# Stick-breaking scores issued in pairs of heads, and a pooling product cut to the band

## The chip, the cores and the metric

The kernel runs on one core of a Trainium2 chip. The metric is the device time of one execution in microseconds (us), lower is better; the number given is the median of several runs. All matrix products are done in a split form: a float32 operand is written as a rounded high part and a low part (`hi`, `lo`), both in the reduced type that TensorE takes, and a product is the sum of three matmuls, high by high, high by low and low by high.

## The reference, cut to what matters

A trunk of four residual layers over 256 tokens of 1024 channels. Each layer has a token mixer (layers 0 and 3: pooling; layer 1: stick-breaking attention; layer 2: a state-space layer called S5), then cross-attention into a fixed memory, then a gated MLP. Two mixers matter here.

```python
def pool_mixer(h, w, scale):          # windows 2, 4, 8, 16 over four channel groups of 256
    for gi, win in enumerate(POOL_WINDOWS):
        win_sum = c - causal_shift(c, win)          # c: running sum over the tokens
        cnt = jnp.minimum(counts, float(win))
        groups.append(win_sum / cnt - hf[..., sl])
    ...
    y = einsum('bsgc,gcd->bsgd', p, w)              # then a per-group linear map and a scale

def stick_breaking_attention(h, w_qkv, w_o):        # 16 heads of 64 channels
    z = einsum('bqhd,bkhd->bhqk', q, k) * scale
    log_one_minus = where(mask, log_sigmoid(-z), 0) # mask: key before query
    between = reverse_cumsum(log_one_minus) - log_one_minus
    a = where(mask, exp(log_sigmoid(z) + between), 0)
    o = einsum('bhqk,bkhd->bqhd', a, v)
```

In the pooling mixer the window mean minus the token is a 256 by 256 matrix over the tokens, one for each window. Column t of it is nonzero only in rows t-15 to t, and its entries are 1/window except in the first 15 columns, where the count is smaller.

## The kernel before, in words

Everything is written as straight code by engine; the framework's scheduler then orders the instructions of each engine by its own estimate of when operands are ready, so code that is near in the program may be interleaved. Each engine runs its own list in order. Weights come from DRAM by `load` (line 79): one DMA of 1 MB into a `raw` tile, then in two halves a cast on ScalarE (ACT, line 70, `whi`) and a subtraction on VectorE (DVE) or, where `eng` says so, on GpSimd (POOL) (line 71, `wlo`). A product `mm3` (line 62) issues three matmuls; in the trace they are lines 65, 66 and 67.

**Pooling, layers 0 and 3** (`pool_mixer`, line 443). The normalised tokens `xh, xl` lie with tokens on the partitions, in two tiles `tt` of 128 tokens. `band` is the matrix above, split like a weight. For each of the four windows and two chunks of 128 channels, two `mm3` (one for each token tile, line 459) of 256 columns sum into half of a PSUM bank: 2 x 2 x 3 matmuls for a window, 48 for a layer. Two `split_scaled` (lines 75 and 76, tiles `ah` on ACT and `al` on DVE) take each bank out. Then 48 matmuls with `pool_w` fill `acc` (line 473), and lines 476 and 477 on DVE scale and add to the residual `h`. In layer 0 two things share the time of this stage: conversions of the convolution constants (lines 145 and 146) and the poles of the S5 layer (a sine and cosine, lines 623 to 657 on DVE in tiny steps, results copied at lines 697 and 698; a power on POOL, line 693). POOL also splits early weights of the cross-attention there.

**Stick-breaking, layer 1** (`stick_mixer`, line 480). Q and K are kept transposed, two heads to a chunk: head 2p in partitions 0 to 63, head 2p+1 in partitions 64 to 127 (`rows`, line 543). For a head, `scores` (line 541) issues six matmuls (line 551: two key tiles by three split terms, 64 rows, 128 stationary and 256 moving columns) into a bank `z`, one matmul that adds the mask (line 552), and then the chain of a head: three activations on ACT (lines 554 to 556), two DVE operations (lines 558 and 559) and a split into `Lh, Ll`. `sticks` (line 563) adds the sums over later keys to `z` with four matmuls (lines 566 and 568), takes the exponential and splits it into `Ah, Al`. `values` (line 573) does six matmuls for a pair of heads (line 581) into `po`. The loop at line 594 runs over head n: `scores(n)`, S5 work at a `fill` point, a projection that a later head needs (the table `order`, 48 matmuls each), `values` at odd n, `sticks(n-1)`. There are two buffers of `Lh, Ll, Ah, Al`, one for even and one for odd heads, and four banks for `z`.

```python
for n in range(SBH + 2):
    if n < SBH:
        zs[n] = scores(n)
    ...
    if n % 2 and n >= 3:
        values((n - 3) // 2)
    if 0 <= n - 1 < SBH:
        sticks(n - 1, zs[n - 1])
```

Of the kernel before, what the change touches and what calls it, by code (L numbers as in the profile page):

```python
# [8 lines left out]
F32 = mybir.dt.float32  # L9
F32R = mybir.dt.float32r  # L10
AF = mybir.ActivationFunctionType
ALU = mybir.AluOpType
AX = mybir.AxisListType

P = 128
T = 256
TT = T // P
# [8 lines left out]
SBH = 16  # L26
# [10 lines left out]
class Trunk:  # L37
# [405 lines left out]
    def pool_mixer(self, l, j, ctx_pool):  # L443
        nc = self.nc
        xs = self.norm_natural()
        xh, xl = self.act_pair(TT, D)
        for tt in range(TT):
            self.split(xh[:, tt, :], xl[:, tt, :], xs[:, tt, :])
        self.fill("mnorm")
        sc = self.bcast(ctx_pool, self.a["pool_scale"][j], "psc")  # L450
        band = self.load(self.a["band"], 8, T)
        ph, pl = self.act_pair()
        for g in range(4):
            ps = self.bank()
            for jj in range(2):
                c = 2 * g + jj
                s = slice(c * P, (c + 1) * P)
                for tt in range(TT):
                    self.mm3(ps[:, jj * T : (jj + 1) * T], (xh[:, tt, s], xl[:, tt, s]), band(2 * g + tt, slice(0, T)), tt == 0, tt == 1)
            for jj in range(2):  # L460
                c = 2 * g + jj
                self.split_scaled(ph[:, c, :], pl[:, c, :], ps[:, jj * T : (jj + 1) * T], self.gain("mix", l, c))
        w = self.load(self.a["pool_w"][j].rearrange("g (c p) n -> p (g c) n", p=P), 8, T)
        self.fill("pool")
        accs = self.accs()
        for gh in range(2):
            for tt in range(TT):
                ps = accs[2 * gh + tt]
                s = slice(tt * P, (tt + 1) * P)
                for gg in range(2):  # L470
                    for k in range(2):
                        c = 4 * gh + 2 * gg + k
                        self.mm3(ps[:, gg * T : (gg + 1) * T], (ph[:, c, s], pl[:, c, s]), w(c, slice(0, T)), k == 0, k == 1)
                t = ctx_pool.tile([P, 512], F32, tag="pt", name="pt", bufs=2)
                cs = slice(512 * gh, 512 * (gh + 1))
                nc.vector.tensor_mul(t[:], ps[:], sc[:, cs])
                nc.vector.tensor_add(self.h[:, tt, cs], self.h[:, tt, cs], t[:])
                self.residual_done(gh, tt, ps[:])

    def stick_mixer(self, l, sp):  # L480
        nc, tc = self.nc, self.tc
        mm = nc.tensor.matmul
# [9 lines left out]
        neg = sp.tile([P, 2 * P], F32R, name="neg")  # L492
        idr = sp.tile([P, P], F32R, name="idr")
# [11 lines left out]
        bufs = []  # L505
# [10 lines left out]
        qk = self.act_pair()  # L516
# [21 lines left out]
            self.split(f(V[0]), f(V[1]), ps[:].rearrange("p (t n) -> p t n", t=TT))  # L538


        def scores(head):
            pair = head // 2
            rows = slice(64 * (head % 2), 64 * (head % 2) + 64)
            qc = 2 * (pair // 2 % 2) + pair % 2
            Lh, Ll = bufs[head % 2][:2]
            z = self.psa.tile([P, 512], F32, tag=f"acc{head % 4}", name="z")
            for kt in (1, 0):
                out = z[:, 0:T] if kt else z[:, T : 2 * T]
                ks = slice(kt * P, (kt + 1) * P)
                for n, (a, b) in enumerate([(0, 0), (0, 1), (1, 0)]):  # L550
                    mm(out, qk[a][rows, 4 + qc, ks], qk[b][rows, qc, :], start=kt == 1 and n == 0, stop=False, skip_group_check=True)
            mm(z[:, P : 3 * P], idr[:], neg[:], start=False, stop=False, skip_group_check=True)
            ab = sp.tile([P, 384], F32, tag="ab", name="ab", bufs=4)
            nc.scalar.activation(ab[:], z[:, P:], AF.Abs, scale=0.125)
            nc.scalar.activation(ab[:], ab[:], AF.Exp, scale=-1.0)
            nc.scalar.activation(ab[:], ab[:], AF.Ln, bias=1.0)
            L = sp.tile([P, 384], F32, tag="ab", name="L", bufs=4)
            nc.vector.tensor_scalar(L[:], z[:, P:], -0.125, 0.0, ALU.mult, ALU.min)
            nc.vector.tensor_sub(L[:], L[:], ab[:])
            self.split(Lh[:, P:], Ll[:, P:], L[:])  # L560
            return z

        def sticks(head, z):
            Lh, Ll, Ah, Al = bufs[head % 2]
            for x in (Lh, Ll):
                mm(z[:, P:], tri[:], x[:, P:], start=False, stop=False, skip_group_check=True)
            for n, x in enumerate((Lh, Ll)):
                mm(z[:, T:], ones[:], x[:, :T], start=False, stop=n == 1, skip_group_check=True)
            A = sp.tile([P, 384], F32, tag="ab", name="A", bufs=4)
            nc.scalar.activation(A[:], z[:, P:], AF.Exp, scale=0.125)  # L570
            self.split(Ah, Al, A[:])

        def values(pair):

            po = self.bank("po")
            cs = slice(P * pair, P * (pair + 1))
            out = po[:].rearrange("p (e q) -> p e q", e=2)

            for kt, q0 in ((0, 0), (1, P)):
                for a, b in ((0, 0), (0, 1), (1, 0)):  # L580
                    mm(
                        out[:, :, q0:], V[a][:, kt, cs], AA[b][:, :, 0:P] if kt else AA[b][:, :, P:],
                        start=kt == 0 and a == b, stop=kt == 1 and a == 1, skip_group_check=True,
                    )
            for e in range(2):
                rows = slice(64 * e, 64 * e + 64)
                self.split(O[0][rows, pair, :], O[1][rows, pair, :], po[rows, T * e : T * (e + 1)])
# [4 lines left out]
        order = {0: "v0", 1: "q1", 3: "k1", 5: "v1", 6: "q2", 7: "k2", 9: "v2", 10: "q3", 11: "k3", 13: "v3"}  # L592
        zs = {}
        for n in range(SBH + 2):
            if n < SBH:
                zs[n] = scores(n)
            self.fill(f"head{n}")
            for unit in order.get(n, "").split():
                u = int(unit[1])
                proj_v(u) if unit[0] == "v" else proj(u, "qk".index(unit[0]))  # L600
            if n % 2 and n >= 3:
                values((n - 3) // 2)
            if 0 <= n - 1 < SBH:
                sticks(n - 1, zs[n - 1])
        self.project(self.a["sb_w_o"][0].rearrange("(c p) n -> p c n", p=P), O, self.add_residual)


# [752 lines left out]
def band():  # L1360

    import numpy as np

    t = np.arange(T)
    out = np.zeros((P, 4, TT, T), np.float32)
    for g, w in enumerate(WINDOWS):
        m = ((t[:, None] <= t[None, :]) & (t[:, None] > t[None, :] - w)) / np.minimum(t + 1, w)[None, :] - np.eye(T)
        out[:, g] = m.reshape(TT, P, T).transpose(1, 0, 2)
    return out.reshape(P, 4 * TT, T).astype(np.float32)
# [31 lines left out]
```

## Time and profile before

| | us |
|---|---|
| median of 3 runs | 1502.92 (1499.14 to 1503.51) |
| the profiled execution | 1504.49 |
| its span | 1502.8 |
| PE busy, of the span | 1436.3 (96%) |
| DVE busy | 1100.1 (73%) |
| ACT busy | 843.0 (56%) |

In the profile PE is TensorE's matmuls, PEld its weight loads, DVE VectorE, ACT ScalarE, POOL GpSimd. The busy time of PE holds the tails of matmuls that overlap the next ones, so what a matmul costs is read from the distance between starts, not from its duration. On the chain that ended last PE has 75% of the span, DVE 12%, DMA 7% and ACT 3%.

### The profile page before, as it was taken

What the parts mean: (1) busy time and instruction counts of PE and PEld (TensorE: products, weight loads), DVE (VectorE), ACT (ScalarE), POOL (GpSimd) and SP (SyncE); (2) the same over time, 40 slices, a digit from 0 to 9 for tenths busy, and PEclk for the clock granted to TensorE, in tenths of its full rate; (3) what the DMA queues carried; (4) which work ended last, traced back from release to release, by engine and by line L of the source; (5) the groups of instructions that cost most, each with busy time, mean ns of one, the idle gap of its engine ahead of it and who ended that gap; (6) DMA issues with size and microseconds to landing.
All of it is one profiled execution on the core that took longest, in us unless ns stands there. A gap on an engine that the chain in (4) does not pass through costs nothing.

```text
span 1502.8 us, 25420 instructions
## 1 busy us (share of the span) xinstructions
PE 1436.3 (96%) x10370; PEld 1325.5 (88%) x10370; DVE 1100.1 (73%) x1720; ACT 843.0 (56%) x1351; POOL 127.1 (8%) x128
## 2 busy tenths in 40 slices
PE   7999999999999999999997679999999999999997
PEld 7898999989998989999986558989999999899996
DVE  6969887867887577978772755868777686677775
ACT  6654656547785465645453245656555565465553
POOL 3401000000000000111116300000000030000000
PEclk9999999999999999999998889999999999999999
DMA  7666656635334645776758474546555464465551
GB/s 257 210 175 208 236 201 208 205 126 184 129 138 144 204 135 194 243 233 218 232 190 241 159 270 151 169 141 226 194 169 196 155 203 163 137 218 179 173 192 43
DMA packets 205682, 279.75 MB, mean 186 GB/s; under 512 B 23740, under 2 KB 163132, under 8 KB 203644
## 3 DMA queue, kind: packets, MB, share of 16 engines
q1 hardware_dynamic: 199420, 263.08, 53.1%
q0 software_dynamic: 6144, 15.04, 3.1%
q8 instruction: 81, 1.33, 0.4%
q14 instruction: 37, 0.30, 0.1%
HBM read 264.24 MB, written 16.94 MB: 187 GB/s over the span
## 4 chain that ended last, share of the span: by engine, by line
PE 75%; DVE 12%; DMA 7%; ACT 3%; issue 2%; SPq 0%; POOL 0%; DVEq 0%; POOLq 0%; ACTq 0%
PE u L66 9%; PE u L67 9%; PE u L65 9%; PE mm L66 7%; PE mm L65 7%; PE mm L67 7%; PE acc L66 6%; PE acc L65 6%; PE acc L67 6%; DMA raw<-in_ffn_w_up_dram 3%; DVE wlo L71 3%; DVE ug L1239 2%; ACT whi L70 1%; DMA raw<-in_s_w_glu_dram 1%; DMA bl<-blD 1%
## 5 line engine op out<-in xcount | busy, mean ns | idle before, releaser
L71 DVE TENSOR_TENSOR wlo<-raw,whi 128x1024 fp32r<-128x1024 f32 x428 | 517.2, 1221 | 157.4 <-ACT whi L70 151.2
L70 ACT CAST whi<-raw 128x1024 fp32r<-128x1024 f32 (+1 forms) x450 | 459.7, 1045 | 194.2 <-DMA raw<-in_ffn_w_up_dram 61.3
L65 PE MATMUL u<-ah,whi 128*128 128x256 f32 x1408 | 400.9, 285 | 2.4 <-DVE ug L1239 2.1
L66 PE MATMUL u<-al,whi 128*128 128x256 f32 x1408 | 400.2, 284 | 0.2 <-DVE al L71 0.2
L67 PE MATMUL u<-ah,wlo 128*128 128x256 f32 x1408 | 400.0, 284 | 0.0
L65 PEld LDWEIGHTS u<-ah,whi 128*128 128x128 f32 x1408 | 271.7, 193 | 6.9 <-issue 3.6
L66 PEld LDWEIGHTS u<-al,whi 128*128 128x128 f32 x1408 | 271.6, 193 | 3.1 <-DVE al L71 0.7
L67 PEld LDWEIGHTS u<-ah,wlo 128*128 128x128 f32 x1408 | 271.7, 193 | 0.0
L1239 DVE SCALAR_TENSOR_TENSOR ug<-u,cwT,ug 128x255 f32<-128x255 f32 x352 | 168.5, 480 | 102.0 <-ACT ug L1237 97.0
L1237 ACT ACTIVATE ug<-u,cwT 128x256 f32<-128x256 f32 x176 | 99.2, 563 | 182.4 <-PE u L67 120.3
L65 PE MATMUL acc<-whi,gg 128*128 128x512 f32 x352 | 138.0, 392 | 0.0
L66 PE MATMUL acc<-wlo,gg 128*128 128x512 f32 x352 | 137.9, 392 | 0.0
L67 PE MATMUL acc<-whi,gg 128*128 128x512 f32 x352 | 136.9, 389 | 0.0
L66 PE MATMUL mm<-al,whi 128*128 128x256 f32 x384 | 109.8, 286 | 0.1
L65 PE MATMUL mm<-ah,whi 128*128 128x256 f32 x384 | 109.7, 286 | 0.0
L67 PE MATMUL mm<-ah,wlo 128*128 128x256 f32 x384 | 109.3, 285 | 0.0
L176 POOL TENSOR_TENSOR r<-v,mhalf 128x1 f32<-128x1 f32 x28 | 21.4, 765 | 832.8 <-DVE v L172 679.4
L67 PEld LDWEIGHTS acc<-whi,gg 128*128 128x128 f32 x352 | 66.1, 188 | 14.3
L65 PEld LDWEIGHTS acc<-whi,gg 128*128 128x128 f32 x352 | 66.4, 189 | 11.7
L66 PEld LDWEIGHTS acc<-wlo,gg 128*128 128x128 f32 x352 | 66.4, 189 | 10.7
L66 PEld LDWEIGHTS mm<-al,whi 128*128 128x128 f32 x384 | 74.4, 194 | 0.8 <-DVE al L71 0.6
L65 PEld LDWEIGHTS mm<-ah,whi 128*128 128x128 f32 x384 | 74.4, 194 | 0.3 <-ACT ah L70 0.2
(348 smaller groups left out, 2605.9 us busy)
## 6 DMA issues: line engine op xcount, KB each, us to landing
raw<-in_ffn_w_up_dram SPq DMA_DIRECT2D x88, 1024.0 KB
raw<-in_ffn_w_down_dram SPq DMA_DIRECT2D x44, 1024.0 KB
raw<-in_xa_wkv_dram SPq DMA_DIRECT2D x30, 1024.0 KB
raw<-in_xa_wq_dram SPq DMA_DIRECT2D x16, 1024.0 KB
raw<-in_xa_wo_dram SPq DMA_DIRECT2D x16, 1024.0 KB
raw<-in_sb_w_qkv_dram SPq DMA_DIRECT2D x12, 1024.0 KB
raw<-in_s_w_glu_dram SPq DMA_DIRECT2D x8, 1024.0 KB
raw<-in_sb_w_o_dram SPq DMA_DIRECT2D x4, 1024.0 KB
```

What stands on the lines that cost most here:

```text
L65: mm(out, lh, rh, start=start, stop=False)
L66: mm(out, lh, rl, start=False, stop=False)
L67: self.multiplied = mm(out, ll, rh, start=False, stop=stop).ins
L70: x = self.nc.scalar.copy(hi, src)
L71: y = (eng or self.nc.vector).tensor_sub(lo, src, hi.bitcast(F32))
L176: self.powed = nc.gpsimd.tensor_tensor(r[:], v[:], self.mhalf[:], ALU.pow).ins
L1237: nc.scalar.activation(u[:, s, :], out, AF.Identity, bias=cw[3], scale=cw[2])
L1239: nc.vector.scalar_tensor_tensor(u[:, s, sh:], out[:, : T - sh], cw[2 - sh], u[:, s, sh:], ALU.mult, ALU.add)
```

## The change

**Pooling.** The three matmuls of 256 columns for each token tile go. For token tile 1 (rows 128 to 255) only columns 128 to 255 are computed, for tile 0 only columns 0 to 143, since the band is zero elsewhere. The product of the tokens with the low part of the band is kept only for the first 16 columns. The matmuls are still in the split form otherwise. A chunk takes 5 matmuls (128, 128, 144, 144 and 16 columns) where there were 6 of 256.

**Stick-breaking.** `scores` works on a pair of heads. It issues the twelve matmuls alternately, one of head 2p on partitions 0 to 63 and one of head 2p+1 on partitions 64 to 127, into two banks; then the mask and the chain of each head. It stops before the split of the second head's `L`, so that `sticks` of the odd head before, which reads the same buffer, is issued first. The loop's even steps hold the scores of two heads, the odd steps none.

```diff
@@ pool_mixer
-                for tt in range(TT):
-                    self.mm3(ps[:, jj * T : (jj + 1) * T], (xh[:, tt, s], xl[:, tt, s]), band(2 * g + tt, slice(0, T)), tt == 0, tt == 1)
+                mm = nc.tensor.matmul
+                for tt, t0, t1 in ((1, P, T), (0, 0, P + 16)):
+                    to = ps[:, jj * T + t0 : jj * T + t1]
+                    bh, bl = band(2 * g + tt, slice(t0, t1))
+                    mm(to, xh[:, tt, s], bh, start=tt == 1, stop=False, skip_group_check=True)
+                    mm(to, xl[:, tt, s], bh, start=False, stop=False, skip_group_check=True)
+                    if t0 == 0:
+                        mm(to[:, 0:16], xh[:, tt, s], bl[:, 0:16], start=False, stop=True, skip_group_check=True)
@@ stick_mixer
-        def scores(head):
-            pair = head // 2
-            rows = slice(64 * (head % 2), 64 * (head % 2) + 64)
+        def scores(pair):
             qc = 2 * (pair // 2 % 2) + pair % 2
-            Lh, Ll = bufs[head % 2][:2]
-            z = self.psa.tile([P, 512], F32, tag=f"acc{head % 4}", name="z")
+            zz = [self.psa.tile([P, 512], F32, tag=f"acc{(2 * pair + e) % 4}", name="z") for e in range(2)]
             for kt in (1, 0):
-                out = z[:, 0:T] if kt else z[:, T : 2 * T]
                 ks = slice(kt * P, (kt + 1) * P)
                 for n, (a, b) in enumerate([(0, 0), (0, 1), (1, 0)]):
-                    mm(out, qk[a][rows, 4 + qc, ks], qk[b][rows, qc, :], start=kt == 1 and n == 0, stop=False, skip_group_check=True)
-            mm(z[:, P : 3 * P], idr[:], neg[:], start=False, stop=False, skip_group_check=True)
+                    for e in range(2):
+                        out = zz[e][:, 0:T] if kt else zz[e][:, T : 2 * T]
+                        rows = slice(64 * e, 64 * e + 64)
+                        mm(out, qk[a][rows, 4 + qc, ks], qk[b][rows, qc, :], start=kt == 1 and n == 0, stop=False, skip_group_check=True)
+            for e, z in enumerate(zz):
+                Lh, Ll = bufs[e][:2]
+                mm(z[:, P : 3 * P], idr[:], neg[:], start=False, stop=False, skip_group_check=True)
...
+                if e:
+                    yield zz
+                self.split(Lh[:, P:], Ll[:, P:], L[:])
@@ the loop over n
-            if n < SBH:
-                zs[n] = scores(n)
+            if n % 2 == 0:
+                rest = scores(n // 2) if n < SBH else iter(())
+                for zs[n], zs[n + 1] in [next(rest, (None, None))]:
+                    pass
+                if n:
+                    sticks(n - 1, zs[n - 1])
+                next(rest, None)
...
-            if n % 2 and n >= 3:
-                values((n - 3) // 2)
-            if 0 <= n - 1 < SBH:
-                sticks(n - 1, zs[n - 1])
+            if n % 2:
+                if n >= 3:
+                    values((n - 3) // 2)
+                if n - 1 < SBH:
+                    sticks(n - 1, zs[n - 1])
```

The order on PE around the second pair's scores, before. `z_4003` and `z_4031` are the banks of heads 2 and 3, `z_3917` that of head 1; `ah` and `al` are the parts of Q and K.

```order
L551 MATMUL z_4003<-ah_3711 128x256
L551 MATMUL z_4003<-al_3712,ah_3711 128x256
L551 MATMUL z_4003<-ah_3711,al_3712 128x256
L552 MATMUL z_4003<-neg_3684,idr_3685 128x256
L566 MATMUL z_3917<-Lh1_3703,tri_3682 128x384
L566 MATMUL z_3917<-Ll1_3704,tri_3682 128x384
L568 MATMUL z_3917<-Lh1_3703,ones_3683 128x256
L568 MATMUL z_3917<-Ll1_3704,ones_3683 128x256
L551 MATMUL z_4031<-ah_3711 128x256
L551 MATMUL z_4031<-al_3712,ah_3711 128x256
L551 MATMUL z_4031<-ah_3711,al_3712 128x256
L552 MATMUL z_4031<-neg_3684,idr_3685 128x256
```

The same place on PE after the change; `z_3995` and `z_3996` are now the banks of heads 2 and 3, `z_3828` that of head 1.

```order
L558 MATMUL z_3995<-ah_3703 128x256
L558 MATMUL z_3996<-ah_3703 128x256
L558 MATMUL z_3995<-al_3704,ah_3703 128x256
L558 MATMUL z_3996<-al_3704,ah_3703 128x256
L558 MATMUL z_3995<-ah_3703,al_3704 128x256
L558 MATMUL z_3996<-ah_3703,al_3704 128x256
L561 MATMUL z_3995<-neg_3676,idr_3677 128x256
L561 MATMUL z_3996<-neg_3676,idr_3677 128x256
L577 MATMUL z_3828<-Lh1_3695,tri_3674 128x384
L577 MATMUL z_3828<-Ll1_3696,tri_3674 128x384
L579 MATMUL z_3828<-Lh1_3695,ones_3675 128x256
L579 MATMUL z_3828<-Ll1_3696,ones_3675 128x256
```

Two blocks of six score matmuls (three of each shown) with the sticks of head 1 between them have become one block of twelve, and the sticks follow it. Over the whole stage the 96 score matmuls stood in 20 blocks (the scheduler had cut four heads in two) and now stand in 12 (four pairs cut in two).

The order on DVE in layer 0, from the end of the S5 poles to the residual, before. `al` is the pooled low part of a chunk, `poles` the S5 results, `cwT` the convolution constants, `pt` and `h` the residual of lines 476 and 477.

```order
L657 TENSOR_TENSOR s5t<-s5t 128x32
L146 COPY cwT<-mm 128x176
L697 COPY poles<-s5t 128x32
L698 COPY poles<-s5t 128x32
L146 COPY cwT<-mm 128x176 x2
L76 SCALAR_TENSOR_TENSOR al<-mm,gT,ah 128x256
L146 COPY cwT<-mm 128x176
L476 TENSOR_TENSOR pt<-acc_646,psc 128x512
L476 TENSOR_TENSOR pt<-acc_647,psc 128x512
L477 TENSOR_TENSOR h<-h,pt 128x512 x2
```

The same place after the change (lines 484 and 485 are the residual now, 714 and 715 the poles, 213 the next norm's gain):

```order
L674 TENSOR_TENSOR s5t<-s5t 128x32
L714 COPY poles<-s5t 128x32
L715 COPY poles<-s5t 128x32
L76 SCALAR_TENSOR_TENSOR al<-mm,gT,ah 128x256
L146 COPY cwT<-mm 128x176 x2
L76 SCALAR_TENSOR_TENSOR al<-mm,gT,ah 128x256 x2
L146 COPY cwT<-mm 128x176 x2
L484 TENSOR_TENSOR pt<-acc_638,psc 128x512
L76 SCALAR_TENSOR_TENSOR al<-mm,gT,ah 128x256
L485 TENSOR_TENSOR h<-h,pt 128x512
L484 TENSOR_TENSOR pt<-acc_639,psc 128x512
L213 TENSOR_TENSOR xs<-h,xs 128x512
```

Four of the eight `al` stand behind the copies of the poles now, where one did, and the residual's additions are spread out. On ACT the four casts of POOL's early weights, which stood behind seven of the eight `ah`, now begin behind four.

## Rows read from the trace of the kernel before

**Rows 1.** The page: TensorE's granted clock in 40 equal slices, in tenths of full speed.

```profile
PEclk9999999999999999999998889999999999999999
```

**Rows 2.** Windows: length; busy us (count) of PE, PEld, DVE, ACT, POOL; clock, DMA, GB/s.

```profile
36.50:42.50 6.00, 6.00 (x52) 6.00 (x52) 5.50 (x35) 2.77 (x6) 4.94 (x1) 1.00 0.98 369
1206.40:1212.20 5.80, 5.80 (x50) 5.80 (x50) 3.30 (x7) 4.50 (x8) 5.80 (x3) 1.00 0.73 250
357.00:462.00 105.00, 105.00 (x750) 96.33 (x750) 81.99 (x131) 83.12 (x159) 1.67 (x3) 1.00 0.41 136
383.10:410.90 27.80, 27.80 (x210) 26.14 (x209) 22.52 (x36) 21.19 (x41) 0.60 (x1) 1.00 0.40 133
410.90:438.70 27.80, 27.80 (x210) 26.13 (x209) 22.04 (x35) 23.85 (x49) 0.53 (x1) 1.00 0.38 133
```

**Rows 3.** Timeline of PE around one head's scores: start, duration, engine, line, operation.

```profile
363.23 0.28 PE L67 MATMUL mm<-whi,al 128*128 128x256 f32 x1
363.44 0.38 PE L551 MATMUL z<-ah 64*128 64x256 f32 x1
363.66 0.28 PE L551 MATMUL z<-al,ah 64*128 64x256 f32 x1
363.78 0.28 PE L551 MATMUL z<-ah,al 64*128 64x256 f32 x1
...
364.13 0.27 PE L551 MATMUL z<-ah,al 64*128 64x256 f32 x1
364.34 0.39 PE L552 MATMUL z<-neg,idr 128*128 128x256 f32 x1
364.56 0.28 PE L65 MATMUL mm<-ah,whi 128*128 128x256 f32 x1
```

**Rows 4.** Timeline of PEld, the weight loads of a later head's first two scores.

```profile
384.45 0.18 PEld L551 LDWEIGHTS z<-ah 64*128 64x128 f32 x1
384.56 0.19 PEld L551 LDWEIGHTS z<-al,ah 64*128 64x128 f32 x1
```

**Rows 5.** Timelines of PE and PEld, 32 matmuls of the S5 layer on alternating row halves.

```profile
618.92 0.67 PE L883 MATMUL mm<-s5g,s5h 64*32 64x128 f32 x32
618.91 0.40 PEld L883 LDWEIGHTS mm<-s5g,s5h 64*32 64x32 f32 x32 [0.35 <-issue]
```

**Rows 6.** Eight transposes of 128 columns by 128: timeline, and their group by line.

```profile
242.58 1.03 PE L820 MATMUL mm<-ident,s5d 128*128 128x128 f32 x8
L820 PE MATMUL mm<-ident,s5d 128*128 128x128 f32 x24 | 3.1, 272 | 0.0
```

**Rows 7.** Timeline of layer 0's pooling (DVE, POOL, PEld) and the stretch after it.

```profile
37.56 5.45 POOL L693 TENSOR_TENSOR poles<-s5t,poles 128x32 f32<-128x32 f32 x1 [12.05 <-DVE poles L692]
44.50 10.01 POOL L71 TENSOR_TENSOR wlo<-raw,whi 128x1024 fp32r<-128x1024 f32 x4 [1.49 <-PE mm L145]
44.87 2.14 DVE L697 COPY poles<-s5t 128x32 f32<-128x32 f32 x1
49.34 5.71 DVE L477 TENSOR_TENSOR h<-h,pt 128x512 f32<-128x512 f32 x2
58.17 0.42 PEld L223 LDWEIGHTS tp<-ident,xs 128*128 128x128 f32 x4 [3.28 <-ACT acc L157]
60.00:63.50 3.50, 3.50 (x10) 2.68 (x10) 3.50 (x7) 0.18 (x1) 2.66 (x2) 0.55 0.02 5
```

**Rows 8.** Timeline of DVE, layer 3's pooling: the first addition to the residual.

```profile
1215.02 2.23 DVE L477 TENSOR_TENSOR h<-h,pt 128x512 f32<-128x512 f32 x1
```

**Rows 9.** Timeline: masks of two heads that follow each other, and their last splits.

```profile
383.72 0.38 PE L552 MATMUL z<-neg,idr 128*128 128x256 f32 x1
385.35 0.39 PE L552 MATMUL z<-neg,idr 128*128 128x256 f32 x1
387.43 0.55 DVE L71 TENSOR_TENSOR Ll<-L,Lh 128x384 fp32r<-128x384 f32 x1
389.62 0.56 DVE L71 TENSOR_TENSOR Ll<-L,Lh 128x384 fp32r<-128x384 f32 x1
```

More of the change, by code (lines that the diff above doesn't have):

```diff
@@ L547, in scores @@
             for kt in (1, 0):
-                out = z[:, 0:T] if kt else z[:, T : 2 * T]
                 ks = slice(kt * P, (kt + 1) * P)
                 for n, (a, b) in enumerate([(0, 0), (0, 1), (1, 0)]):
-                    mm(out, qk[a][rows, 4 + qc, ks], qk[b][rows, qc, :], start=kt == 1 and n == 0, stop=False, skip_group_check=True)
-            mm(z[:, P : 3 * P], idr[:], neg[:], start=False, stop=False, skip_group_check=True)
-            ab = sp.tile([P, 384], F32, tag="ab", name="ab", bufs=4)
@@ L554, in scores @@
[L554 to L561, printed above, removed]
+                    for e in range(2):
+                        out = zz[e][:, 0:T] if kt else zz[e][:, T : 2 * T]
+                        rows = slice(64 * e, 64 * e + 64)
+                        mm(out, qk[a][rows, 4 + qc, ks], qk[b][rows, qc, :], start=kt == 1 and n == 0, stop=False, skip_group_check=True)
@@ new lines, in scores @@
+            for e, z in enumerate(zz):
+                Lh, Ll = bufs[e][:2]
+                mm(z[:, P : 3 * P], idr[:], neg[:], start=False, stop=False, skip_group_check=True)
+                ab = sp.tile([P, 384], F32, tag="ab", name="ab", bufs=4)
+                nc.scalar.activation(ab[:], z[:, P:], AF.Abs, scale=0.125)
+                nc.scalar.activation(ab[:], ab[:], AF.Exp, scale=-1.0)
+                nc.scalar.activation(ab[:], ab[:], AF.Ln, bias=1.0)
+                L = sp.tile([P, 384], F32, tag="ab", name="L", bufs=4)
+                nc.vector.tensor_scalar(L[:], z[:, P:], -0.125, 0.0, ALU.mult, ALU.min)
+                nc.vector.tensor_sub(L[:], L[:], ab[:])
+                if e:
+                    yield zz
+                self.split(Lh[:, P:], Ll[:, P:], L[:])
```

## The prediction

> **What bounds the kernel now.** I read the busy times and the clock of the page first, then windows of the two stages that the change touches, then timelines inside them. TensorE is at full clock in nearly all slices [rows 1]. In the stick-breaking stage, 357 to 462, PE is busy for all of its 105 us, with DVE and ACT at 82 and 83 [rows 2]. So this stage is as long as the starts of its matmuls, and a start taken out is time taken out, as long as DVE and ACT can follow. In both poolings PE issues a matmul about every 0.116 us (50 in 5.80) [rows 2], but what follows them differs: layer 0 ends in a wait of PE for the residual [rows 7]; layer 3 shows PE busy throughout [rows 2].
>
> **Scores.** Inside a head's block the matmuls of 256 columns start 0.118 us apart (363.66 to 364.13 is four steps) [rows 3]. Entering the block, from matmuls on all 128 rows to matmuls on 64, costs two longer steps, 0.21 and 0.22, and leaving it again 0.21 and 0.22 [rows 3]. Against four steps of 0.12 that is 0.38 us for a block. The change has 12 blocks where there were 20: 8 x 0.38 = 3.0 us.
>
> The larger term is whether a matmul on the lower half of the rows and one on the upper half share their time. No row shows it for these tiles. The nearest is line 883 of the S5 layer, whose code alternates the two halves of the rows too (on 32 columns at a time): its 32 matmuls and the 32 weight loads ahead of them all start within 0.67 us, tail included [rows 5]. One after the other at 0.118 they would take 3.8 us. The bounds are 0.118 us for two matmuls (they overlap fully) and 2 x 0.118 (they don't). I take the first: of all rows only line 883 has this alternation, and its loads overlap as well as its matmuls. 96 matmuls become 48 slots, 48 x 0.118 = 5.7 us. Together 8.7 us off PE in this stage.
>
> What takes some of it back. The mask matmuls, the sticks, the values and the projections are the same in number and length; they only stand elsewhere. Two heads now enter ACT and DVE at once. For two heads in a row the masks lay 1.6 us apart and the last splits 2.2 us (387.43 and 389.62) [rows 9], so the second split of a pair comes about 2.2 us after the first, which itself ends 3.9 us after its mask (384.10 to 387.98): 6.1 us. In most pairs 48 or 96 projection matmuls (5.7 us or more) and the values lie between, and no one waits. At the last pair only 15 matmuls of the output projection (0.23 us each by their 512 columns, an estimate of twice 0.116), about 3.5 us, and the sticks of two heads (1.2 us) do; I put 0.8 us of waiting there, between 0 and 1.5. Over the other pairs the stage gets 8% shorter while DVE's work stays: 22.5 of 27.8 us becomes 22.5 of 25.6, ACT 23.9 of 25.6 in the fuller stretch [rows 2]. Both still fit; for waits in between I put 0.6 us, with 5 us as the bad end (a rival below). Stage: 8.7 - 0.8 - 0.6 = **7.3 us**.
>
> **Pooling.** Six matmuls of 256 columns for a chunk become five of 128, 128, 144, 144 and 16. The price can't fall with the columns: each has its own load of 128 weights, and the next load starts 0.11 us after the one before (384.45, 384.56) [rows 4]. Eight transposes of 128 by 128 show what that makes: (1.03 - 0.27) / 7 = 0.109 us apart [rows 6], hardly less than the 0.116 of 256 columns. The bounds are that 0.109, and half of 0.116, 0.058, if the columns alone counted. I take 0.109, since the transposes have the same load: 48 x 0.116 - 40 x 0.109 = 1.2 us for a layer, 2.4 for both. The page "TensorE: Matmul & The Clock Gate" of the Trainium skill, under "Back-to-back issue gap", gives about 81 ns for pairs of load and matmul of 128 columns; by that the two layers would save 2.2 us more. Our transposes at 0.109 speak against it.
>
> Layer 3 has PE busy before and after, so I let 1.0 of its 1.2 us through; the addition to the residual, 2.23 us where the others take 0.7 [rows 8], is held up by POOL's subtractions, which don't move, and may eat the rest. In layer 0 PE stands still for 3.28 us later, until the residual is there [rows 7]: what counts is DVE. It is held by POOL's four subtractions from 44.5 to 54.5, in whose time a copy took 2.14 us and two additions 5.71 [rows 7]. In the changed order ACT prepares POOL's first weights after four `ah`, not seven, so POOL can begin once its power is done at 43.0 [rows 7], 1.5 us earlier, and end so much earlier. Against that, DVE's copies of the poles now stand ahead of four `al` that the next product waits for, and one more addition may fall under a subtraction (2.4 us). Bounds: 1.5 us gained plus the 1.4 us that the half clock after the wait costs (ten matmuls in 3.5 us at a mean 0.55, where 0.23 each is usual) [rows 7], to 2.4 lost. I take 0.8 gained. Pooling: 1.0 + 0.8 = **1.8 us**. No DMA and nothing on POOL or SP changes its place; the order of both queues is the same.
>
> **Sum.** 7.3 + 1.8 = 9.1 us. On the profiled execution 1504.49 - 9.1 = 1495.4. That execution lies 1.6 us above the median of the runs, so the median goes from 1502.9 to **1493.8**. The rest of the kernel has the same order and simply starts earlier. Its own range, with the score term between 6 and 8.7 and pooling between 0 and 4.5, is 1490 to 1497.
>
> **Rivals.**
> (1) The halves don't overlap. Then only the switches go, 3.0 us, the pair's chains are closer to PE's pace, and 3.0 - 0.8 + 1.8 = 4.0: 1498.9. For it: the loads on line 883 are of 32 columns, these of 128, and they might follow each other at 0.11 [rows 4]. Against it: there, too, loads and matmuls of both halves start together [rows 5]. The same page of the Trainium skill (Part 2, step 1) has one read port for weights and one for the moving operand, by which the loads of both halves would queue; line 883's loads, 32 within 0.40 us, don't look like it. Chance 0.10.
> (2) DVE and ACT become the bound of the stick-breaking stage. In-order queues near 90% make PE wait 0.5 to 1 us for a pair's `Ll` or `Ah`; eight pairs give back 4 to 8 us, and 8.7 - 0.8 - 6 + 1.8 = 3.7: about 1499. For it: ACT at 23.9 of 27.8 [rows 2]. Against: a head's chain ends 4 us after its mask, and the projection ahead of its use is longer. Chance 0.10.
> (3) Slower. Every change of half costs what a change of block costs, about 0.10 us a step [rows 3]. A pair's block would take 12 x 0.22 + 0.19 = 2.83 us where its two blocks took 2 x (0.71 + 0.38) = 2.18, so 0.65 lost on each of eight pairs, 5.2; with 1.3 of waits and 1.8 gained in pooling 1507.6. It decides from 0.04 us a step on, where the blocks saved are used up. Against it: line 883 alternates at every matmul and shows no such step [rows 5]. "TensorEngine Tiling" (Key Properties) in the Trainium skill says that a change of mode drains the engine and one of tile within a mode does not; the steps at the ends of the block agree with the first half. Chance 0.05.
> (4) Layer 0's order goes wrong, DVE stuck behind POOL with `al` in its queue: 3 to 4 us lost there, 1498 to 1500. Chance 0.04.
>
> **How the numbers follow.** The forecast has 0.71. About 0.3%, 4.5 us, is what a measurement of this kernel tells from no change, so faster means under 1498.4. The forecast counts there almost whole (0.70), of rivals 1, 2 and 4 a third (0.08): 0.78. Same 0.16 from the rest of these three, slower 0.06 from rival 3 and a worse case of 2. The range from 1488 to 1501 holds the forecast with room for pooling at 0.058 us a matmul, and rivals 1, 2 and 4; rival 3 and the far end of 2 are left out.
>
> **What would show it.** Right: in the profile after, the twelve matmuls of line 558 start in couples some 0.01 us apart, couples 0.12 apart, a block of them with its ends is near 1.1 us, and the five pooling matmuls of a chunk start 0.11 apart. PE's stage from the first score to the last value is 7 us shorter. Wrong: starts at an even 0.12 (rival 1) or 0.22 (rival 3); waits of PE for `Lh`, `Ll` or `Ah` in every pair (rival 2); a wait of PE in layer 0 that ends later than 58.2 us (rival 4).

## The result and the profile after

The median goes from 1501.36 us (5 runs) to 1493.65 (1491.77 to 1494.47, 5 runs): a ratio of 0.9938, 95% interval 0.9924 to 0.9953, or 9.3 us by the ratio (7.1 to 11.4; the two medians alone differ by 7.7). The change timed once more gave 0.9937 (0.9916 to 0.9958). The profiled execution took 1494.25 us, with a span of 1492.5 (before 1502.8). 1493.8 was forecast. The total is right; its two parts are not: nearly all of it comes from the scores, and pooling gives nothing that the timed runs can tell from zero.

Windows of after, with the columns of [rows 2]. The first two are the repeating piece of two pairs, 25.7 and 25.6 us where [rows 2] had 27.8, with the same number of matmuls. The third and fourth hold the two poolings' band products, the fifth and sixth layer 0 behind it, the last the second product of layer 3's pooling.

```profile
377.10:402.80 25.70, 25.70 (x210) 24.55 (x208) 21.96 (x36) 20.84 (x40) 0.60 (x1) 1.00 0.43 143
402.80:428.40 25.60, 25.60 (x209) 24.55 (x208) 21.51 (x35) 22.95 (x48) 0.53 (x1) 1.00 0.38 131
36.10:41.00 4.90, 4.66 (x43) 4.57 (x41) 4.76 (x27) 1.84 (x4) 3.21 (x1) 1.00 0.84 254
1195.90:1200.60 4.70, 4.70 (x45) 4.70 (x44) 2.33 (x4) 3.57 (x6) 4.67 (x2) 1.00 0.83 274
42.50:49.30 6.80, 5.39 (x25) 5.13 (x26) 5.00 (x20) 5.70 (x9) 6.02 (x4) 0.51 0.31 124
60.00:63.50 3.50, 3.50 (x22) 2.95 (x20) 3.50 (x6) 0.85 (x3) 2.31 (x2) 1.00 0.10 26
1200.50:1207.70 7.20, 7.05 (x50) 6.09 (x50) 5.03 (x10) 4.80 (x10) 5.49 (x3) 1.00 0.52 174
```

**The scores.** The timeline of PE around one pair's block, which answers to [rows 3]; a row of scores with x2 is a couple whose two starts lie 1 to 6 ns apart.

```profile
367.66 0.28 PE L579 MATMUL z<-Ll,ones 128*128 128x256 f32 x1
367.87 0.38 PE L558 MATMUL z<-ah 64*128 64x256 f32 x2
368.10 0.28 PE L558 MATMUL z<-al,ah 64*128 64x256 f32 x2
368.21 0.28 PE L558 MATMUL z<-ah,al 64*128 64x256 f32 x2
...
368.57 0.28 PE L558 MATMUL z<-ah,al 64*128 64x256 f32 x2
368.77 0.51 PE L561 MATMUL z<-neg,idr 128*128 128x256 f32 x2
369.12 0.34 PE L577 MATMUL z<-Lh,tri 128*128 128x384 f32 x1
```

Twelve matmuls take the room of six (367.87 to 368.57 is 0.70 us; 363.44 to 364.13 in [rows 3] was 0.69), and the longer steps at the ends, 0.21, 0.23 and 0.20, are as before. Their loads start in couples too, on PEld:

```profile
367.87 0.18 PEld L558 LDWEIGHTS z<-ah 64*128 64x128 f32 x2
367.98 0.19 PEld L558 LDWEIGHTS z<-al,ah 64*128 64x128 f32 x2
```

In [rows 4] two loads lay 0.11 apart. From the first score to the first transposes behind the stage PE took 119.8 us before (357.66 to 477.48) and takes 111.8 (355.61 to 467.37): 8.1 us. The second head's last split on DVE lies 0.7 to 3.7 us behind the first's in the eight pairs; the pair shown has 2.0, where [rows 9] had 2.2 for two heads in a row:

```profile
409.33 0.55 DVE L71 TENSOR_TENSOR Ll<-L,Lh 128x384 fp32r<-128x384 f32 x1
411.34 0.55 DVE L71 TENSOR_TENSOR Ll<-L,Lh 128x384 fp32r<-128x384 f32 x1
```

**Layer 0's pooling.** Timeline rows of the four engines, which answer to [rows 7].

```profile
39.70 0.48 DVE L76 SCALAR_TENSOR_TENSOR al<-mm,gT,ah 128x256 fp32r<-128x256 f32 x1
40.22 0.84 ACT L75 ACTIVATE ah<-mm,gT 128x256 fp32r<-128x256 f32 x2 [2.29 <-DVE al L76]
42.02 0.39 PE L145 MATMUL mm<-ident,rows 88*128 88x88 f32 x2 [1.26 <-issue]
42.53 0.47 ACT L75 ACTIVATE ah<-mm,gT 128x256 fp32r<-128x256 f32 x1 [1.48 <-DVE al L76]
43.65 0.53 PE L145 MATMUL mm<-ident,rows 88*128 88x88 f32 x2 [1.24 <-DVE s5t L673]
44.02 9.88 POOL L71 TENSOR_TENSOR wlo<-raw,whi 128x1024 fp32r<-128x1024 f32 x4 [0.78 <-ACT whi L70]
49.08 2.56 DVE L485 TENSOR_TENSOR h<-h,pt 128x512 f32<-128x512 f32 x1
58.36 1.03 PE L223 MATMUL tp<-ident,xs 128*128 128x128 f32 x8
```

The band is done in 4.4 us (36.15 to 40.55 in starts) and not 5.7, and PE then stands for some 1.3 us twice, ahead of the transposes of the convolution constants (line 145), which by the program need one of the four PSUM banks that the band has filled. A bank waits for its second `al`, `al` stands in DVE's queue among the sine and cosine steps, and ACT's next `ah` of the same bank starts only when DVE's `al` on it is done (40.22 behind 39.70 plus 0.48). PE's clock falls to half from 42.5 to 49.3 (0.51), and the `tp` come at 58.36, where [rows 7] had a wait that ended at 58.17. What layer 0 got is that the half clock of [rows 7] at 60 to 63.5 is gone (1.00 for 0.55): it has moved ahead of the `tp`, into a stretch where PE has waits anyway.

**Layer 3's pooling.** The band is 1.3 us shorter here too (4.3 for 5.6 in starts), and the product behind it, 48 matmuls, is 1.3 longer: 7.2 us, the last window above, where it had taken 5.9 before:

```profile
1212.10:1218.00 5.90, 5.90 (x52) 5.90 (x51) 5.21 (x8) 3.92 (x7) 4.35 (x2) 1.00 0.59 188
```

The waits of after in 1200 to 1208 (who, for what, total us, times, longest) say why: `ah` and `al` wait for each other, and PE for both.

```profile
DVE al L76 <- ACT ah L75: 2.7, 4, 0.8
ACT ah L75 <- DVE al L76: 1.7, 3, 0.6
...
PEld acc L67 <- DVE al L76: 0.6, 3, 0.2
PEld acc L65 <- ACT ah L75: 0.5, 2, 0.3
```

### The profile page after: what moved, and what is told of

Its sections match the earlier page's. It is cut to its first block, busy times and chain, and to the rows that moved or that the text cites. A ratio compares the mean times of both kernels' runs of the same rounds, so it can differ in the third digit from the quotient of the medians.

```text
span 1492.5 us, 25390 instructions
## 1 busy us (share of the span) xinstructions
PE 1426.9 (96%) x10354; PEld 1317.2 (88%) x10354; DVE 1093.6 (73%) x1720; ACT 839.8 (56%) x1351; POOL 127.2 (9%) x128
## 4 chain that ended last, share of the span: by engine, by line
PE 76%; DVE 11%; DMA 7%; ACT 3%; issue 2%; SPq 1%; POOL 0%; DVEq 0%; POOLq 0%; ACTq 0%
PE u L66 9%; PE u L67 9%; PE u L65 9%; PE mm L65 7%; PE mm L66 7%; PE mm L67 7%; PE acc L65 7%; PE acc L66 7%; PE acc L67 7%; DMA raw<-in_ffn_w_up_dram 3%; DVE wlo L71 3%; DVE ug L1256 1%; ACT whi L70 1%; DMA bl<-blD 1%; DVE h L434 1%
## 5 line engine op out<-in xcount | busy, mean ns | idle before, releaser
L70 ACT CAST whi<-raw 128x1024 fp32r<-128x1024 f32 (+1 forms) x450 | 460.0, 1045 | 192.6 <-DMA raw<-in_ffn_w_up_dram 58.2
L65 PE MATMUL acc<-whi,ah 128*128 128x512 f32 (+1 forms) x192 | 73.0, 380 | 1.9 <-ACT whi L70 1.7
```

The costliest lines, as they stand in the source:

```text
L65: mm(out, lh, rh, start=start, stop=False)
L70: x = self.nc.scalar.copy(hi, src)
```

## Experiments

Each ratio is to the kernel before, timed on the same chip; the us are 1502 times its distance from 1. The stage columns come from PE's starts in the one profiled execution: **A** from the first score to the first transposes of the cross-attention behind it, **B** from the first band matmul of layer 0 to the fifth of the eight `tp` (in two kernels the first four come apart), **D** from the same band matmul to the first `tp` of layer 0's MLP, **C** from the first `tp` of layer 2's MLP to that of layer 3's cross-attention.

| kernel | ratio, 95% interval | us | A | B | D | C |
|---|---|---|---|---|---|---|
| before | | | 119.8 | 22.2 | 100.3 | 223.0 |
| the change | 0.9938 (0.9924 to 0.9953) | -9.3 | 111.8 | 22.6 | 99.1 | 223.1 |
| the change again | 0.9937 (0.9916 to 0.9958) | -9.5 | 111.7 | 22.3 | 98.7 | 223.0 |
| pooling alone | 0.9998 (0.9989 to 1.0007) | -0.3 | 119.8 | 21.5 | 97.9 | 223.0 |
| scores alone | 0.9935 (0.9921 to 0.9948) | -9.8 | 111.8 | 22.5 | 99.9 | 223.0 |
| halves in turn | 0.9934 (0.9919 to 0.9949) | -9.9 | 112.9 | 22.2 | 98.6 | 223.0 |
| band at full width | 0.9943 (0.9929 to 0.9956) | -8.6 | 111.7 | 23.4 | 99.9 | 223.0 |
| both heads on one half | 0.9971 (0.9956 to 0.9986) | -4.4 | 117.0 | 22.1 | 98.5 | 223.1 |
| mask between the halves | 0.9989 (0.9975 to 1.0002) | -1.7 | 119.1 | 22.4 | 98.8 | 223.1 |
| low part of the keys first | 0.9931 (0.9907 to 0.9954) | -10.4 | 109.2 | 22.6 | 99.0 | 223.0 |
| sine and cosine later | 0.9930 (0.9909 to 0.9951) | -10.5 | 111.8 | 20.5 | 97.0 | 223.0 |
| three edits | 0.9927 (0.9906 to 0.9948) | -11.0 | 109.2 | 20.4 | 98.5 | 222.2 |
| three edits, DVE for POOL | 0.9917 (0.9896 to 0.9937) | -12.5 | 109.2 | 19.1 | 94.9 | 224.0 |
| the best parts | 0.9872 (0.9856 to 0.9889) | -19.2 | 109.2 | 19.2 | 95.0 | 222.2 |

A and C repeat within 0.1 us from run to run where the code is the same, while whole runs of one kernel spread over 5 to 10 us. B and D spread by 0.6 over the six kernels whose code up to there is the change's (B 22.1 to 22.6, D 98.5 to 99.1). Pooling alone, with the same pooling code, lies lower; PE's clock is at half from 45.3 to 48.7 there, from 42.7 to 49.5 in the change. So an edit is read in its stage, and the total only says whether it arrives.

### The two parts apart

Pooling alone is the kernel before with the change's part of `pool_mixer`, scores alone with its parts of `stick_mixer` (the two halves of the diff above).

> The kernel before with the new pooling loop alone. Theory: TensorE's 40 matmuls take 4.5 us a layer instead of 5.8 in both layers, but nothing of it reaches the end of layer 3's pooling (the first transposes `tp` there start within 0.3 us of their old distance from the band), because the bank-by-bank exchange of ACT's `ah` and DVE's `al` sets the pace; what is gained comes from layer 0 alone, through a half-clock stretch that moves away from 59.7: 1 to 2 us off the whole. Rival A, the prediction's own: 0.8 from layer 0 and 1.0 from layer 3, with `tp` in layer 3 a full 1 us nearer to the band. Rival B: the whole of the 2.5 us that TensorE saves is off the time. Rival C: nothing or slower, and the gain of the change is in the scores alone.

> The change with the old pooling loop. Theory: the stick-breaking stage alone is worth 8 us (from the first score to the last value), so 7 to 8.5 us off the time of before, and with the run of the new pooling loop alone the two sum to the change's 9 to 10. Rival: parts interact, through the places where the clock falls; then the two sums differ by over 1.5 us.

Pooling alone: -0.3 us (-1.7 to 1.1), rival C. Stage C stays at 223.0, as the theory had it. In layer 0 B is 0.7 shorter. B ends ahead of the stretch at half clock that [rows 7] showed, so D says more: 97.9 with pooling alone and 98.5 to 99.1 in the kernels with the change's layer 0, for 100.3 before and 99.9 with scores alone, so 0.8 to 2.4 us are gained by the start of layer 0's MLP; that the half clock that moved is the reason is argued, not shown. The timed runs don't show a gain at the end, and one of up to 1.7 us stays possible. Scores alone: -9.8 (-11.9 to -7.8), all of the change and above the 7 to 8.5 expected, with A at 111.8; A accounts for 8.1 of it, and the rest is within the interval. The sum of the parts, -10.1, is within the intervals of the change's -9.3; no interaction shows.

### The price of a band matmul

```diff
-                for tt, t0, t1 in ((1, P, T), (0, 0, P + 16)):
+                for tt, t0, t1 in ((1, 0, T), (0, 0, T)):
```

> The change with the four large band matmuls of a chunk at all 256 columns, where the change has 128 and 144: still five matmuls a chunk. Theory: the price of a matmul is its load's, not its columns': the band takes 4.5 to 4.8 us a layer here too. Rival A: columns count, and the band takes 0.3 us or more a layer longer than in the change for every 0.01 us by which a step of 256 columns exceeds one of 128. This width also leaves ACT and DVE in the order of the kernel before in layer 0 (`al` among the sine and cosine steps earlier); by the theory TensorE then doesn't wait 1.5 us twice at the transposes of the convolution constants, and the time is within 1.5 us of the change on either side, by where the clock falls.

The kernel was not quite what its expectation says: with both tiles starting at column 0, the piece of 16 columns is issued for both, six matmuls a chunk, 48 a layer. That makes a cleaner test: 16 of the 48 have 16 columns where the kernel before has 256. The timeline of PE in layer 3:

```profile
1197.13 0.36 PE L464 MATMUL mm<-whi,ah 128*128 128x256 f32 x1
1197.33 0.28 PE L465 MATMUL mm<-whi,al 128*128 128x256 f32 x1
1197.45 0.17 PE L467 MATMUL mm<-wlo,ah 128*128 128x16 f32 x1
1197.47 0.36 PE L464 MATMUL mm<-whi,ah 128*128 128x256 f32 x1
```

Three take 0.35 us in the rows that follow, 0.116 each, the 16-column one included: what its own step saves (0.03) the next one pays (0.20). In starts the band takes 5.6 and 5.5 us in the two layers, where the 48 of 256 took 5.7 and 5.6 before (0.120 each): sixteen matmuls cut from 256 columns to 16 save 0.17 us, 0.01 each. The change's 40 take 4.4 and 4.3, 0.11 each. The price is that of a load and matmul, nearly whatever the columns up to 256. And C is 223.0 with a band of 5.5 us and 223.1 with one of 4.3: layer 3 doesn't wait for it. In layer 0 the first transposes of line 145 follow the band at once (42.60), as expected, but PE stands 3.5 us later for DVE's copies `cwT` (until 49.91), and B is 23.4.

### Is it the alternation?

Six matmuls of the lower half, then six of the upper, all else in the same order on every engine but PE:

```diff
-            for kt in (1, 0):
+            for e, kt in ((0, 1), (0, 0), (1, 1), (1, 0)):
                 ks = slice(kt * P, (kt + 1) * P)
                 for n, (a, b) in enumerate([(0, 0), (0, 1), (1, 0)]):
-                    for e in range(2):
```

> The change with the twelve score matmuls of a pair issued as six of the lower half and then six of the upper half, all else in the same order. Theory: the overlap of two halves is worth 48 x 0.118 = 5.7 us and goes; the blocks saved, 3 us or less, stay: 5 to 6 us slower than the change, 3.5 to 4.5 faster than before. Rival A: it's the pairing and the order of the queues that gain, not the alternation: within 1 us of the change. Rival B: the chip overlaps the halves at the one place where they meet only, and each return to the other half costs 0.1: slower than the change by 6.5 or more.

The theory fell: -9.9, the same as the change, and A is only 1.1 us longer. The timeline of PE shows what happened to a block of six and six:

```profile
368.17 0.38 PE L557 MATMUL z<-ah 64*128 64x256 f32 x1
368.40 0.28 PE L557 MATMUL z<-al,ah 64*128 64x256 f32 x1
368.51 0.28 PE L557 MATMUL z<-ah,al 64*128 64x256 f32 x1
368.52 0.39 PE L557 MATMUL z<-ah 64*128 64x256 f32 x2
368.74 0.28 PE L557 MATMUL z<-al,ah 64*128 64x256 f32 x2
368.86 0.28 PE L557 MATMUL z<-ah,al 64*128 64x256 f32 x2
368.98 0.28 PE L557 MATMUL z<-ah 64*128 64x256 f32 x1
369.10 0.28 PE L557 MATMUL z<-al,ah 64*128 64x256 f32 x1
369.21 0.28 PE L557 MATMUL z<-ah,al 64*128 64x256 f32 x1
```

The program has ah; al,ah; ah,al twice for the lower half and then the same for the upper. The rows don't come in that order: the two `ah` at 368.52 stand together, though two others lie between them in the program. Two matmuls of one half start 0.11 apart, so what starts 0.01 after the third lower one is the first upper one, the seventh of the program. The built program's list for PE has the six lower ones and then the six upper ones, so it isn't the scheduler that mixes them: TensorE runs ahead by itself, to a matmul four places on, and the block takes 1.04 us where the alternating one takes 0.70 and one after the other would take 1.41. In blocks of four and four (four of the eight pairs are cut in 4 and 8) it overlaps wholly: 379.38 to 379.84. So the alternation itself is worth three steps in four blocks, 12 x 0.116 = 1.4 us; A says 1.1. The Trainium skill, "TensorE: Matmul & The Clock Gate", Part 3, The mechanism, says "MATMULs are pc-monotone in start AND end"; these rows differ, and the measurement decides: matmuls on different halves of the rows leave the program's order. The sentence ahead of the prediction that each engine runs its own list in order doesn't hold for them.

Two runs then had to tell whether it is an overlap at all. First the upper half was taken away; then, in the kernel of six and six, a matmul on all rows was put between the halves:

```diff
-                        rows = slice(64 * e, 64 * e + 64)
+                        rows = slice(0, 64)
```

```diff
+                if kt == 0:
+                    mm(zz[e][:, P : 3 * P], idr[:], neg[:], start=False, stop=False, skip_group_check=True)
...
-                mm(z[:, P : 3 * P], idr[:], neg[:], start=False, stop=False, skip_group_check=True)
```

> The change with both heads of a pair on the lower half of the rows (the odd head's scores are left out and the even head's computed twice, with matmuls of the same number and size in the same order). Theory: the gain in the scores is made of an overlap on the chip, which needs the two halves and not their strict alternation, and of 8 blocks fewer. Without the overlap 48 steps of 0.116 come back: 5.6 us slower than the change, 3 to 4 faster than before; the matmuls of a block start at an even 0.116. Rival: the overlap in the profile is only a matter of how starts are recorded, and the gain is that of order and queues: within 1 us of the change.

> The change with six matmuls of the lower half, its mask, six of the upper half, its mask. The mask is a matmul on all 128 rows, so nothing of the upper half can run ahead past it. Theory: both parts go except in the four pairs' first pieces that are cut from the rest (two and two matmuls without a mask between); four of 12 blocks are whole and four are cut in 4 and 8, so 8 more blocks (8 x 0.38 = 3.0) and 40 of 48 steps (40 x 0.116 = 4.6): 7 to 8 us slower than the change, within 1.5 us of before. Rival: the mask doesn't hold the next block back, and it is within 2 us of the change.

Both as the theory had it. With both heads on one half (the odd heads' own scores left out), in the same order and number, the kernel stands at -4.4, 4.9 us above the change; A is 5.2 longer, and the couples are gone (two starts of `z<-ah` in 0.50 us, where a couple took 0.38):

```profile
368.65 0.50 PE L558 MATMUL z<-ah 64*128 64x256 f32 x2
368.99 0.39 PE L558 MATMUL z<-al,ah 64*128 64x256 f32 x2
```

With the mask between, -1.7, and A at 119.1 is 0.7 under before. Nothing of the upper half passes the mask:

```profile
370.34 0.27 PE L557 MATMUL z<-ah,al 64*128 64x256 f32 x1
370.54 0.38 PE L559 MATMUL z<-neg,idr 128*128 128x256 f32 x1
370.86 0.38 PE L557 MATMUL z<-ah 64*128 64x256 f32 x1
371.08 0.28 PE L557 MATMUL z<-al,ah 64*128 64x256 f32 x1
```

### What the change left

In four pairs of the change the block is cut in 4 and 8, since the low part of the keys, split last, isn't ready for the third couple. With that product first, a block waits once and runs whole:

```diff
-                for n, (a, b) in enumerate([(0, 0), (0, 1), (1, 0)]):
+                for n, (a, b) in enumerate([(1, 0), (0, 0), (0, 1)]):
```

> The change with the low part of the keys as the first of the three products, not the last. That operand is ready last where a projection has just been split, and in the change four pairs of eight are cut for it into blocks of 4 and 8. Theory: a block costs 0.38 whatever it holds, 12 blocks become 8, and 4 x 0.38 = 1.5 us come off in the stage, less than 0.5 of it given back in waits for that operand. Rival: the cut was cover: TensorE now waits for the operand (DVE's split comes some 0.7 us behind ACT's) four times, and the time is that of the change or up to 1.5 us more.

-10.4 in the total, whose interval holds the change's; the stage is clear. A is 2.5 us shorter. Of these about 1.0 is only where A begins: the first score now stands behind eight matmuls of the projection (8 x 0.12) that were behind it. The other 1.5 are the four blocks saved, as forecast. A block that was cut:

```profile
378.06 0.39 PE L558 MATMUL z<-ah,al 64*128 64x256 f32 x2
...
378.97 0.51 PE L561 MATMUL z<-neg,idr 128*128 128x256 f32 x2
```

In layer 0 the sine and cosine were moved from `s5_poles` to `s5_start`, in the MLP; the angle waits in the tile `poles`:

```diff
-        th = tm(0)
-        v.tensor_mul(th, dt, lim)
-        s1, c1 = self.sincos(th, [tm(i) for i in range(2, 10)])
-        v.tensor_copy(sn, s1)
-        v.tensor_copy(cs, c1)
+        v.tensor_mul(sn, dt, lim)
...
+        s1, c1 = self.sincos(self.poles[:, 0, :], [tm(i) for i in range(2, 10)])
+        v.tensor_copy(self.poles[:, 0, :], s1)
+        v.tensor_copy(self.poles[:, 1, :], c1)
         self.s5_ratio(tm)
```

> The change with the 34 steps of sine and cosine for the S5 poles moved from layer 0's pooling to the S5 preparation in layer 0's MLP. Theory: in the pooling these steps hold up DVE's `al`, one bank's `al` holds up its next `ah` on ACT, the banks come free late, and TensorE stands 1.5 us twice at the transposes of the convolution constants; without them the transposes start by 41.5 and 42.5, DVE has 4 us less ahead of the residual, and the first `tp` of layer 0 starts 2 to 3 us earlier than in the change (58.2). Of that 1 to 3 us are left at the end. Rival A: POOL's four subtractions, which end at 53.9 and hold the additions, decide: `tp` within 0.5 us of the change. Rival B: the steps cost as much in the MLP, where DVE is 70 to 80% busy: no gain at the end.

B is 1.6 to 2.2 shorter than in the change and its repeats, D 1.5 to 2.1, between theory and rival A; the total's 1.2 lies within the intervals. PE's waits at line 145 shrink: the first four of its transposes start at 41.56, and no half clock comes before 141 us. What comes next is POOL (the first four `tp` start at 54.77, the other four wait):

```profile
43.45 10.41 POOL L71 TENSOR_TENSOR wlo<-raw,whi 128x1024 fp32r<-128x1024 f32 x4
...
51.52 2.88 DVE L485 TENSOR_TENSOR h<-h,pt 128x512 f32<-128x512 f32 x1
...
57.55 0.63 PE L223 MATMUL tp<-ident,xs 128*128 128x128 f32 x4 [2.19 <-DVE xs L213]
```

An addition that takes 0.68 alone takes 2.9 beside POOL's subtractions. Two more kernels followed. The first has the two edits above and queues the last of ACT's four casts of the early weights behind the last `ah`; the second, on top of it, splits these weights on DVE:

```diff
-            with self.behind(*after):
+            with self.behind(*after, *(late if i else ())):
                 for j in range(0, h, n):
...
+            if kind == "v" and l % 3 == 0 and h == 1:
+                kw["late"] = self.last[:1]
```

```diff
-                self.plan((l, "pool"), l, "+v0g")
+                self.plan((l, "pool"), l, "+v0")
```

> The change with three edits: the low part of the keys first, the sine and cosine later, and in layers 0 and 3 the last of ACT's four casts for the early weights of the cross-attention queued behind the last `ah`. Theory: the edits add: 1.1 to 1.5 us in the scores, 0.8 in layer 0 (where POOL's subtractions now decide), and in layer 3, where a cast of 1.0 us stands between two `ah`, 0.5 to 1 us sooner for the first `tp`; 2.5 to 3.5 us below the change. Rival: in layer 3 the `tp` comes 0.3 us sooner at most, because POOL's last subtraction (2.4 us) starts later with its cast and the weights are late; then 1.5 to 2 below the change.

> The kernel of the three edits with the early weights of the cross-attention in layers 0 and 3 split by DVE, not by POOL. Theory: POOL's subtractions take 2.5 us each and hold DVE's additions, which take 2.3 to 2.9 us there instead of 0.7; without them DVE has 4 x 1.2 = 4.9 us more to do and 5.6 (layer 0) and 0.5 (layer 3) less to wait: layer 0's `tp` comes 0.5 to 1.5 us sooner, layer 3's 3 to 4 us later, and the kernel is 2 to 3 us slower than with the three edits. Rival: DVE has room in both layers, and the kernel gains 1 to 3 us on the three edits.

The late cast gives 0.9 in C (222.2; the other two edits left C at 223.0), so ACT's cast between two `ah` was part of layer 3's bound, as the theory had it; the total, -11.0, is 1.5 under the change where 2.5 to 3.5 were expected. Part of what is missing is in layer 0: B is shorter, but D is that of the change, since PE's clock is at half behind the first `tp`, as it was before:

```profile
58.20:61.60 3.40, 3.40 (x10) 2.64 (x9) 3.40 (x5) 0.30 (x1) 2.66 (x2) 0.50 0.03 2
```

DVE in POOL's place gives 1.3 more in B, as the theory had it, and 3.6 more in D, where no half clock stands; it costs 1.8 in layer 3, not 3 to 4. By D and C that kernel is 1.8 us ahead; the totals, -11.0 and -12.5, can't be told apart. So the last kernel takes DVE in layer 0 (`"+v0"`) and POOL in layer 3 (`"+v0g"`):

> The three edits, with the early weights split by DVE in layer 0 alone and by POOL in layer 3. Theory: each layer behaves as it did alone: 19.5 us from the band to the last `tp` of layer 0, 89.1 from the first to the last score, 222.2 from one `tp` of layer 2's MLP to that of layer 3's cross-attention; 1.8 us below the kernel with POOL off in both layers, 3.5 to 5 below the change. Rival: what is gained in layer 0 is given back as half clock or in the MLP, and it isn't below the kernel with POOL off by the trace's stages.

Its stages are those of the parts, 109.2, 19.2 (D 95.0) and 222.2, and no half clock comes back in layer 0; there the additions run at their own pace, two in 1.29:

```profile
53.71 1.29 DVE L487 TENSOR_TENSOR h<-h,pt 128x512 f32<-128x512 f32 x2
...
56.24 1.03 PE L223 MATMUL tp<-ident,xs 128*128 128x128 f32 x8
```

It is faster than the change beyond the intervals: 0.9872 (0.9856 to 0.9889) against 0.9937 (0.9916 to 0.9958). The stages explain 1.6 (A, without the 1.0 of its later start) + 4.1 (D) + 0.9 = 6.6 us; the spans of the two profiled executions differ by as much (1485.9 and 1492.5), the ratios by 9.7, twice what was expected. The 3 us between aren't explained: this kernel and the change weren't timed side by side.

How far such comparisons can be set beside each other was asked with the change once more, beside the two kernels of three edits:

> The change itself once more, beside the two above on one chip. Theory: 0.9935 to 0.9945 of before. Rival: the comparison of separate chips shifts the ratio by over 0.0015, and differences of 1 us between the experiments can't be told.

0.9937 for 0.9938, so the theory; but the intervals are 2 to 3 us wide on either side, and differences of 1 us stay with the stages.

## Why the prediction was right, and where it wasn't

- **The overlap, 48 x 0.118 = 5.7.** Right in kind and size: taken away, it costs 5.2 us in the stage and 4.9 in the total. The reason was too narrow. Line 883 was chosen because it alternates [rows 5]; what counts is that the halves stand within four matmuls of each other. Nothing in the trace of before could show that, since a mask on all rows lay between any two heads.
- **Eight blocks fewer, 3.0.** Right: blocks went from 20 to 12, and four more saved gave 1.5, 0.38 each, once the 1.0 of A's later start is taken off.
- **What the stage gives back, 0.8 + 0.6.** Too much: A lost 8.1 of 8.7, so 0.6 was given back. The forecast for the stage was 7.3. The first term was right: at the last pair PE's loads wait 0.6 and 0.3 us for `Lh` and `Ll` (444.2 and 445.2), where one wait of 0.25 stood before. The second was nothing: between the other pairs no wait is longer than 0.2.
- **A pooling matmul at 0.109.** Right to 0.004 (0.111 and 0.113 in the two layers; a matmul of 256 columns took 0.120 there and not 0.116, so a band saves 1.3 us and not 1.2), and the bound of 0.058 is out: even 16 columns come hardly cheaper. The 81 ns for 128 columns of the Trainium skill ("TensorE: Matmul & The Clock Gate", Back-to-back issue gap) weren't seen in any run here: 0.11 us.
- **"Layer 3 has PE busy before and after, so I let 1.0 of its 1.2 us through."** Wrong: 0, with a band of 5.5 us or of 4.3. A PE that is busy throughout was taken for a PE that bounds. Its pace there was also that of `ah` and `al`, which take about half a microsecond each on one bank in turn; the shorter band turned 1.3 us of it into waits.
- **"I take 0.8 gained" in layer 0.** POOL began 0.5 us earlier, not 1.5 (44.02 for 44.50), and counted from the band's first matmul 0.0 to 0.6 (7.9 and 7.3 us in the change's two executions, 7.9 before); the `tp` came no sooner counted from the band (B is 22.6 and 22.3, and 22.2 before). The copies and steps of the sine and cosine ahead of `al` were named as the risk; they held `al`, the banks and PE, as the run without them showed. What the change gained there (D is 1.2 to 1.6 shorter) fits a half clock that moved, and the timed runs can't tell it from zero. The bound of 1.4 for that half clock doesn't come out of its own numbers either: 3.5 less ten times 0.23 is 1.2.
- **The rivals.** Rivals 1 and 3 would show as starts at an even 0.12 or 0.22, and there are couples, of the loads of 128 columns too. Rival 2 would show as waits in every pair, and the longest wait of PE's loads for `Lh` is 0.6 us, once. Rival 4's sign, a wait in layer 0 that ends later than 58.2, was just met (the `tp` at 58.36), but its 3 to 4 us weren't lost: D is shorter. What held `al` was the sine and cosine ahead of it on DVE, not POOL.

So 8.1 from the scores' stage and about 0 from pooling stand where 7.3 and 1.8 were forecast; two misses of opposite sign made the sum fit. That is luck, and so is 1493.8 beside 1493.65: the forecast took 9.1 from a median of 1502.9, while the two medians compared here differ by 7.7.

## What to carry to other kernels

An engine that is busy all through a stage isn't thereby its bound: before a saving on it is let through, look at how fast the engines behind it take its results out of PSUM, here `ah` and `al` in turn on one bank. Matmuls on half the rows are paired with those of the other half by keeping them within a few places of each other with no full-row matmul between; strict alternation adds little. For small edits compare a stage's length, which repeats to 0.1 us where the clock doesn't fall in it, end the stage behind any stretch at half clock that the edit can move, and let timed runs say only whether it arrives.

## What was unexpected of the hardware

- Matmuls on the two halves of the rows start out of the program's order, an upper one beside a lower one that stands four places before it: 368.51 and 368.52, in a block whose program has three more lower ones between them. Six places was not seen.
- A matmul of 16 columns costs nearly as much as one of 256 when each has its own load of 128 columns: 0.116 us on average with every third one of 16 columns, 0.120 with none.
- A single mask on all rows between two blocks costs as much as a whole block does among full-row matmuls: its three long steps (0.20 into it, 0.31 out of it and 0.22 behind the first score) are 0.38 above three plain ones of 0.12.
